# A trunk of two layers on one core: raw weights, the place of a mean and the staging of the output in the last projection

## The chip, the core and the metric

The kernel runs on one core of a Trainium2 chip. The metric is the device time of one execution in microseconds (us). It is given as the median of three runs, beside the span of one profiled execution, which is the time from its first instruction to its last.

## What is computed

The reference is a trunk of two residual layers over 512 tokens with 16 meta tokens in front, D = 2048, all in float32. Layer 0 holds a convolution module beside sparse attention, layer 1 a gated linear recurrence with 16 heads. The change lies in the end of layer 1 and in the last norm. Cut to that:

```python
o = hgrn2_chunkwise(q, log_f, k, v)                 # 16 heads of 128
o = o * rsqrt(mean(o*o, -1) + 1e-6) * norm_g        # per head
o = o.reshape(b, t, 2048) * silu(g)                 # g = hn @ w_in's last quarter
h = h + o @ w_out                                   # the output projection
return rms_norm(h, final_norm_gain)[:, 16:]         # over D, meta tokens dropped
```

## The kernel before

Everything is kept transposed, with 128 channels on the partitions and tokens along the free dimension. A product in float32 accuracy is made from three matmuls: weights and activations are each split into a high part (rounded, made by ScalarE with an activation) and a low part (the rest, made by VectorE with a subtraction), and high x high, low x high and high x low go into the same PSUM tile. `products` (L170) issues these for eight contraction steps of 128: L174, L175 and L176.

**Weights.** `load_half` (L140) brings 128 x 1024 raw weights (512 KB) into a tile `w32` from the queue of SP, splits it into `wh` (L146, ScalarE) and `wl` (L147, VectorE) and returns both. There are two buffers of `w32` and three each of `wh` and `wl`. In the trace `w32` is named `w`.

**Layer 1's gate.** The loop at L968 makes 16 stripes of the gate (`stripe(S_G + h)`), and multiplies each head's result `ON[h]` by it (`gate_on`, L937). A head's tile holds 512 tokens, seen as two halves of 256 (HS).

**The output projection by Strassen's scheme.** The 2048 x 2048 projection is done for pairs `pr` of output tiles n0 = 2 pr and n1 = 2 pr + 1, over two halves of the contraction (heads 0 to 7 and 8 to 15) and two halves of the tokens, c = 0 and 1. The scheme (Winograd's variant) takes seven products instead of eight: m = 1 to 7. Each product has its own weights (a slice of w, or a sum of slices, `wsum`, that was made in DRAM earlier) and its own form of the activations, named in FORM (L911): B11, B21 and N1 are split early, as the gate proceeds (`early_form`, L919, tiles `eh` and `el`, 28 buffers each); N2 for heads 4 to 7, T3, B22 and T4 are split late (`late_form`, L924) into the tiles `xh` and `xl` that held layer 1's input, and N2 for heads 0 to 3 early. A head's `ON` tile is read by the late forms last.

**The turns.** The list `turns` (L1039) has 56 entries (pr, m). A turn is one product: 24 matmuls of 256 columns into one PSUM tile (`mps` or `s1`, which the trace calls `s`), whose weights come from `weights` (L979). The first ten turns are (0, 1), (0, 5), (0, 2), (0, 6), (1, 1), (1, 5), (0, 7), (0, 3), (0, 4), (1, 2); pairs 6 and 7 alternate at the end with m = 1, 6, 7, 2, 4, 5, 3, so the last six turns are (6, 4), (7, 4), (6, 5), (7, 5), (6, 3), (7, 3). With m = 1 the two residual tiles `H2[n0]` and `H2[n1]` (256 KB each) are loaded from DRAM (L1050) into the ring `on` of 16 buffers that held ON. After each product VectorE adds it to H2 (`add`, L989; m = 6 and 7 go through a sum U).

**Norm and output.** When a tile's half is complete, `finish` (L993) squares it on ScalarE (L1003), adds the square to `acc2` (named `rstd` in the trace, L1005), and scales the tile by the gain (L1006). When the 16th tile of a token half is done, `final` (L1010) is called at once: a matmul with a matrix of 1/D over `acc2` and one over the last square (L1016, L1017, in plain float32) give the mean in every partition; ScalarE makes Ln and Exp (L1019, L1021) after a table load (L1014); VectorE multiplies the 16 tiles (L1033) into staging tiles, and SP sends these out (L1034). The first half (c = 0) stages in pieces of two tiles through `gt2` (two buffers, named `gt`); the second in pieces of 4, 4, 4, 2, 2 in buffers of `w32`, `wh` and `wl`.

**What sets the order.** Each engine and each DMA queue takes its instructions in the order of the program. This order is made when the kernel is built, by a planner with a timeline of its own: among what it holds to be ready it takes the highest level first (`band`: weights 5, evacuation 4, side work 3, products 0). `tc.issue_after(i)` keeps instructions of the engine of `i` behind `i`. A tile's buffer is taken again when all its readers are done.

Of the kernel before, what the change touches and what calls it, by code (L numbers as in the profile page):

```python
# [10 lines left out]
F32 = mybir.dt.float32  # L11
F32R = mybir.dt.float32r
# [6 lines left out]
SEQ = 512  # L19
NM = 16  # L20
T = SEQ + NM
HT = T // 2
D = 2048
KT = D // 128
# [48 lines left out]
def trunk_kernel(ctx: ExitStack, tc: tile.TileContext, x: bass.AP, w: bass.AP, wukv: bass.AP,  # L73
# [3 lines left out]
    V, S, G, P, Q = nc.vector, nc.scalar, nc.gpsimd, nc.tensor, nc.sync  # L77

    def band(level):
        return tc.high_priority(level * 1000000)  # L80

    WGT, EVAC, SIDE, CONV = 5, 4, 3, 2

    consts = ctx.enter_context(tc.tile_pool(name="consts", bufs=1, side="left"))
    wpool = ctx.enter_context(tc.tile_pool(name="wpool", bufs=3, side="left"))
# [7 lines left out]
    def ps1():  # L93
        return side_ps.tile([128, 512], F32, name="s1", bufs=4)
# [15 lines left out]
    def ones_of(val, name):  # L110
        t = cst([128, 128], F32, name)
        V.memset(t, val)
        return t

    ones_d = ones_of(1.0 / D, "ones_d")
# [21 lines left out]
        V.tensor_scalar(vec[:, V_RG:V_RG + 16], vec[:, V_RG:V_RG + 16], 0.5, None, op0=OP.mult)  # L137


    def load_half(src, pool=wpool, names=("wh", "wl"), bufs=3, m=128):  # L140
        w32 = wpool.tile([128, 1024], F32, name="w32", bufs=2)
        Q.dma_start(w32, src)
        hi = pool.tile([128, 1024], F32R, name=names[0], bufs=bufs)
        lo = pool.tile([128, 1024], F32R, name=names[1], bufs=bufs)
        used, uh, ul = [t.rearrange("p (k m) -> p k m", m=128)[:, :, :m] for t in (w32, hi, lo)]
        S.activation(uh, used, AF.Copy)  # L146
        V.tensor_tensor(ul, used, uh.bitcast(F32), op=OP.subtract)  # L147
        return hi, lo
# [20 lines left out]

    def products(o, hi, lo, X, start, stop, m=128):  # L170

        for k, (xh, xl) in enumerate(X):
            ws = slice(k * 128, k * 128 + m)
            P.matmul(o, hi[:, ws], xh, start=start and k == 0, stop=False)  # L174
            P.matmul(o, hi[:, ws], xl, start=False, stop=False)  # L175
            P.matmul(o, lo[:, ws], xh, start=False, stop=stop and k == 7)  # L176

    def evac(dst, parts, rstd):
        o = T - dst.shape[-1]
# [58 lines left out]
    last = {}  # L238
# [64 lines left out]
    for k in range(KT):  # L303
        xh, xl = X0[k]
        st, sp = k == 0, k == KT - 1
        for parts, s, m in ((kwp, S_KW, KWM), (c0p, S_C, 128)):
            hi, lo = first[s, k // 8]
            ws = slice(k % 8 * m, k % 8 * m + m)
# [5 lines left out]
    with band(EVAC):  # L314
        for k in range(KT):
# [5 lines left out]
            else:  # L321
                sq = et([128, T], F32, "sq", 3)
# [13 lines left out]
    for j in range(2):  # L336
        ps = c0p if j == 0 else stripe(S_C + 1, X0, got=first, ring=(ps1, ps1))
        c = et([128, T], F32, "gb", 2)
        with band(EVAC):
            evac(c, ps, rstd0)  # L340
        with band(SIDE):
            sq = et([128, T], F32, "sq", 3)
# [4 lines left out]
    with band(SIDE):  # L347
        p = ps1()
# [16 lines left out]
    with band(SIDE):  # L365
# [7 lines left out]
        for o in range(0, BL, 352):  # L373
# [3 lines left out]
            p = ps1()  # L377
# [48 lines left out]
    for t in range(NB):  # L426
        m = et([128, wk(t)], F32, f"mask{t}", 1)
# [170 lines left out]
    for step in EVEN:  # L598
        what, i = step[0], int(step[1:])
# [34 lines left out]
    r2p = r2.__enter__()  # L634
# [5 lines left out]
    for n in range(KT):  # L640
# [4 lines left out]
        with band(EVAC):  # L645
# [6 lines left out]
            else:  # L652
                sq = U.tile([128, T], F32, name="sq1", bufs=2)
                last = S.activation(sq, hin, AF.Square)
# [16 lines left out]
    def ht(shape, dt, name, bufs=1):  # L671
        return (hp if name == "on" else hrp).tile(shape, dt, name=name, bufs=bufs)
# [225 lines left out]
    fp = ctx.enter_context(tc.tile_pool(name="fp", bufs=2, side="left", reuse_waits="tile"))  # L898
    HS = SEQ // 2
# [11 lines left out]
    FORM = {1: "B11", 2: "B21", 3: "B22", 4: "T4", 5: "N1", 6: "N2", 7: "T3"}  # L911
    forms = {f: [None] * 8 for f in FORM.values()}
# [4 lines left out]
        V.tensor_tensor(lo, src, hi.bitcast(F32), op=OP.subtract)  # L917

    def early_form(name, i, src):  # L919
        hi, lo = [fp.tile([128, HS], F32R, name=n, bufs=28) for n in ("eh", "el")]  # L920
        split2(hi, lo, src)
        forms[name][i] = hi, lo

# [10 lines left out]
    def gt2():  # L934
        return fp.tile([128, 2 * SEQ], F32, name="gt2", bufs=2)
# [22 lines left out]
    def forms_of_both(i):  # L958

        a, b, aj, bj = quarters(i)  # L960
        early_form("B21", i, aj)
        V.tensor_tensor(b, bj, b, op=OP.subtract)
        V.scalar_tensor_tensor(a, b, -1.0, a, op0=OP.mult, op1=OP.subtract)
        if i < 4:
            early_form("N2", i, a)
        V.scalar_tensor_tensor(aj, a, -1.0, aj, op0=OP.mult, op1=OP.subtract)

    for i in range(8):  # L968
# [3 lines left out]
                forms_of(i)  # L972
    with band(SIDE):
        for name in ("N2", "T3", "B22", "T4"):
            for i in range(4 if name == "N2" else 0, 8):
                late_form(name, i)


    def weights(pr, m):  # L979

        n = S_OO + 2 * pr
        src = {1: w[n, 0], 2: w[n, 1], 4: w[n + 1, 1]}[m] if m in (1, 2, 4) else wsum[pr, m]
        return load_half(src)

    H2 = [None] * KT
    acc2 = r2p.tile([128, T], F32, name="rstd1", bufs=1)[:, :SEQ]
    done = [0, 0]

    def add(n, c, ps, op=OP.add):  # L989
        h2 = H2[n][:, c * HS:(c + 1) * HS]  # L990
        V.tensor_tensor(h2, h2, ps, op=op)

    def finish(n, c):  # L993

        cs = slice(c * HS, (c + 1) * HS)
        h2, a2 = H2[n][:, cs], acc2[:, cs]
        done[c] += 1
        sq = last = None
        if done[c] == 1:
            S.activation(a2, h2, AF.Square)  # L1000
        else:
            sq = tmp()
            last = S.activation(sq, h2, AF.Square)  # L1003
            if done[c] < KT:
                V.tensor_tensor(a2, a2, sq, op=OP.add)  # L1005
        S.activation(h2, h2, AF.Identity, scale=col(V_GF + n))  # L1006
        if done[c] == KT:
            final(c, sq, last)

    def final(c, sq, last):  # L1010
        tk = slice(c * HS, (c + 1) * HS)
        if c == 0:
            with tc.issue_after(last.ins):
                S.preload_act_table_set("natural_log_exp_and_others")  # L1014
        p = ps1()[:, :HS]
        P.matmul(p, ones_d, acc2[:, tk], start=True, stop=False)  # L1016
        P.matmul(p, ones_d, sq, start=False, stop=True)  # L1017
        rs = tmp()
        S.activation(rs, p, AF.Ln, bias=eps_r)  # L1019
        rsp = ps1()[:, :HS]  # L1020
        S.activation(rsp, rs, AF.Exp, scale=-0.5)  # L1021
        with band(0 if c else SIDE - EVAC):
            at = 0
            for g, size in enumerate((4, 4, 4, 2, 2) if c else (2,) * 8):
                if c == 0:
                    o = gt2()
                elif g < 2:
                    o = wpool.tile([128, 1024], F32, name="w32", bufs=2)
                else:
                    o = wpool.tile([128, 1024], F32R, name=("wh", "wl", "wh")[g - 2], bufs=3).bitcast(F32)  # L1030
                o = o[:, :size * HS].rearrange("p (n t) -> p n t", n=size)
                for i in range(size):
                    V.tensor_tensor(o[:, i, :], H2[at + i][:, tk], rsp, op=OP.mult)  # L1033
                Q.dma_start(out[at:at + size, :, tk].rearrange("n p t -> p n t"), o)  # L1034
                at += size


    TWO = 6
    turns = [(pr, m) for pr in range(TWO) for m in (1, 5, 2, 6, 7, 3, 4)]  # L1039
    turns[4:9] = [(1, 1), (1, 5), (0, 7), (0, 3), (0, 4)]  # L1040
    turns += [(pr, m) for m in (1, 6, 7, 2, 4, 5, 3) for pr in (6, 7)]

    U = {}
    for at, (pr, m) in enumerate(turns):
        n0, n1 = 2 * pr, 2 * pr + 1
        if m == 1:
            with band(EVAC):
                for n in (n0, n1):
                    H2[n] = ht([128, SEQ], F32, "on", 16)
                    Q.dma_start(H2[n], h1d[n, :, NM:])  # L1050
        o = (mps if at % 7 < 3 else ps1)()[:, :HS]
        with band(WGT):
            hi, lo = weights(pr, m)
        products(o, hi, lo, forms[FORM[m]], True, True)
        with band(EVAC):
            if m == 1:
                u = U[pr] = fp.tile([128, HS], F32, name="u", bufs=2)
                S.activation(u, o, AF.Copy)
                add(n0, 0, o)
            elif m == 5:  # L1060
                add(n0, 1, o)
                add(n1, 1, o, OP.subtract)
                if pr >= TWO:
                    finish(n1, 1)
            elif m == 2:
                add(n0, 0, o)
                finish(n0, 0)
            elif m == 6:
                V.tensor_tensor(U[pr], U[pr], o, op=OP.add)
                add(n0, 1, U[pr])  # L1070
            elif m == 7:
                V.tensor_tensor(U[pr], U[pr], o, op=OP.add)
                h2 = H2[n1].rearrange("p (c t) -> p c t", c=2)
                V.tensor_tensor(h2, h2, U[pr][:, None, :].to_broadcast([128, 2, HS]), op=OP.subtract)
                if pr < TWO:
                    finish(n1, 1)
            elif m == 3:
                add(n0, 1, o)
                finish(n0, 1)
            else:  # L1080
                add(n1, 0, o, OP.subtract)
                finish(n1, 0)
    r2.__exit__(None, None, None)


# [88 lines left out]
```

## Time and profile before

| | us |
|---|---|
| median of three runs (lowest to highest) | 1967.5 (1965.49 to 1968.01) |
| the profiled execution, its own time | 1964.9 |
| its span | 1962.4 |
| TensorE busy | 1931.9 |
| VectorE busy | 1355.2 |
| ScalarE busy | 846.4 |

How to read it: the span is 2.5 us shorter than the execution's own time, which includes what lies around the first and the last instruction. Busy is the time in which an engine runs at least one instruction; matmuls overlap, so two of them can start 0.12 us apart and each last 0.28 us. Times in the rows below are counted from the span's start. The projection's turns begin at 1766.9 us.

### The profile page before, as it was taken

How to read it: one execution, taken by the hardware profiler on the slowest of the kernel's cores; microseconds unless marked ns; L12 is line 12 of the kernel's file. 1: busy time of each engine (PE TensorE's matmuls, PEld its weight loads, DVE VectorE, ACT ScalarE, POOL GpSimd, SP SyncE). 2: the span in 40 equal slices, each digit the busy share in tenths (PEclk: the TensorE clock that was granted, in tenths of full speed). 3: DMA queues.
4: the chain of work that ended last, by engine and by line, in shares of the span. 5: the costliest groups of instructions: out<-in, count | busy, mean ns of one | idle time of the engine just before them, and what ended most of it. 6: DMA issues, size and time to landing. Idle time of an engine off the chain costs nothing.

```text
span 1962.4 us, 36435 instructions
## 1 busy us (share of the span) xinstructions
PE 1931.9 (98%) x14998; PEld 1818.5 (93%) x14998; DVE 1355.2 (69%) x2581; ACT 846.4 (43%) x1475; POOL 119.4 (6%) x202
## 2 busy tenths in 40 slices
PE   9999999999999999999999999999999999999996
PEld 8999899999999999999999999999999988889995
DVE  6699989987376454344777777777777756557665
ACT  6332442234435433233455545454545443345443
POOL 1000000111120100001001000010000000000000
PEclk9999999999999999999999999999999999999998
DMA  6322323334342443434445444344444422235554
GB/s 210 108 83 95 102 88 105 104 99 131 101 115 87 115 137 132 141 135 152 136 130 140 125 123 119 119 140 128 131 119 119 119 76 97 97 118 205 173 172 161
DMA packets 77270, 244.59 MB, mean 125 GB/s; under 512 B 9712, under 2 KB 17432, under 8 KB 76592
## 3 DMA queue, kind: packets, MB, share of 16 engines
q1 hardware_dynamic: 62624, 194.21, 29.4%
q0 software_dynamic: 14192, 47.86, 10.9%
q8 instruction: 118, 1.93, 0.4%
q14 instruction: 48, 0.39, 0.1%
q10 hardware_dynamic: 288, 0.19, 0.0%
HBM read 223.12 MB, written 44.78 MB: 137 GB/s over the span
## 4 chain that ended last, share of the span: by engine, by line
PE 73%; DMA 5%; DVE 3%; ACT 2%; issue 1%; ACTq 0%; DVEq 0%
PE mps L176 21%; PE mps L174 21%; PE mps L175 21%; DMA w<-ws 3%; DMA w<-in_w_dram 2%; ACT wh L146 1%; DVE wl L147 1%; PE po L547 1%; PE s L522 1%; PE s L716 1%; PE s L715 1%; PE s L717 1%; PE po L838 1%; PE po L837 1%; PE s L834 1%
## 5 line engine op out<-in xcount | busy, mean ns | idle before, releaser
L174 PE MATMUL mps<-xh,wh 128*128 128x264 f32 (+2 forms) x3492 | 1070.6, 307 | 3.9 <-DVE gt L181 2.2
L176 PE MATMUL mps<-xh,wl 128*128 128x264 f32 (+2 forms) x3492 | 1072.2, 307 | 0.1
L175 PE MATMUL mps<-xl,wh 128*128 128x264 f32 (+2 forms) x3492 | 1070.3, 307 | 0.1
L174 PEld LDWEIGHTS mps<-xh,wh 128*128 128x128 f32 x3492 | 658.4, 189 | 33.5 <-DVE gt L181 2.2
L175 PEld LDWEIGHTS mps<-xl,wh 128*128 128x128 f32 x3492 | 657.3, 188 | 30.5 <-issue 0.6
L176 PEld LDWEIGHTS mps<-xh,wl 128*128 128x128 f32 x3492 | 657.4, 188 | 28.0 <-DVE wl L147 0.5
L146 ACT ACTIVATE wh<-w 128x1024 fp32r<-128x1024 f32 x313 | 331.5, 1059 | 608.6 <-PE mps L175 452.8
L147 DVE TENSOR_TENSOR wl<-w,wh 128x1024 fp32r<-128x1024 f32 x313 | 382.8, 1223 | 229.7 <-ACT wh L146 224.7
L492 DVE SCALAR_TENSOR_TENSOR z<-u,vec,z 128x528 f32<-128x528 f32 x240 | 180.5, 762 | 2.6
L181 DVE TENSOR_TENSOR gt<-mps,rstd 128x264 f32<-128x264 f32 (+1 forms) x80 | 38.5, 482 | 74.1 <-PE mps L176 73.1
L711 ACT ACTIVATE qhm<-q 128x256 f16<-128x256 f32 x128 | 51.8, 417 | 56.4 <-DVE q L813 44.2
L798 DVE COPY_PREDICATED A<-msk,s 128x256 f32<-128x256 uint8 x96 | 46.5, 484 | 28.3 <-PE s L717 27.8
L176 PE MATMUL s<-xh,wl 128*128 128x256 f32 (+1 forms) x220 | 63.0, 286 | 1.2 <-DVE wl L147 1.1
L712 DVE SCALAR_TENSOR_TENSOR qlm<-q,qhm 128x256 f16<-128x256 f32 x128 | 52.9, 424 | 15.8 <-ACT qhm L711 15.7
L174 PE MATMUL s<-xh,wh 128*128 128x256 f32 (+1 forms) x220 | 62.2, 283 | 0.3 <-ACT wh L146 0.3
L175 PE MATMUL s<-xl,wh 128*128 128x256 f32 (+1 forms) x220 | 62.0, 282 | 0.0
L176 PE MATMUL mps<-eh,wl 128*128 128x256 f32 x156 | 45.2, 290 | 1.8 <-DVE wl L147 1.6
L457 ACT ACTIVATE sq<-s 128x264 f32<-128x264 f32 (+3 forms) x80 | 29.2, 393 | 38.9 <-PE s L455 32.3
L647 DVE TENSOR_TENSOR hin<-mps,hin 128x264 f32<-128x264 f32 x32 | 13.8, 433 | 46.4 <-PE mps L176 46.4
L711 ACT ACTIVATE kt1h<-k 128x256 f16<-128x256 f32 x64 | 26.5, 414 | 44.4 <-DVE k L804 44.4
L174 PE MATMUL mps<-eh,wh 128*128 128x256 f32 x156 | 44.2, 283 | 0.4 <-ACT wh L146 0.4
L823 ACT ACTIVATE kk<-s 128x512 f32<-128x512 f32 x16 | 9.6, 600 | 81.1 <-PE s L821 81.1
(356 smaller groups left out, 2600.8 us busy)
## 6 DMA issues: line engine op xcount, KB each, us to landing
w<-in_w_dram SPq DMA_DIRECT2D x283, 512.0 KB, 3.7
ws<-in_w_dram POOLq DMA_DIRECT2D x48, 512.0 KB, 5.6
w<-ws SPq DMA_DIRECT2D x32, 512.0 KB, 3.6
ws<-ws POOLq DMA_DIRECT2D x16, 512.0 KB, 5.1
hin<-in_x_dram SPq DMA_DIRECT2D x16, 264.0 KB, 3.7
h1d<-hin SPq DMA_DIRECT2D x16, 264.0 KB, 2.1
on<-h1d SPq DMA_DIRECT2D x16, 256.0 KB, 4.7
z<-in_x_dram SPq DMA_DIRECT2D x8, 264.0 KB, 4.6
```

The costliest lines, as they stand in the source:

```text
L146: S.activation(uh, used, AF.Copy)
L147: V.tensor_tensor(ul, used, uh.bitcast(F32), op=OP.subtract)
L174: P.matmul(o, hi[:, ws], xh, start=start and k == 0, stop=False)
L175: P.matmul(o, hi[:, ws], xl, start=False, stop=False)
L176: P.matmul(o, lo[:, ws], xh, start=False, stop=stop and k == 7)
L181: V.tensor_tensor(dst[:, sl.start - o:sl.stop - o], p[:dst.shape[0]], rstd[:dst.shape[0], sl], op=OP.mult)
L457: S.activation(r[:, :s1 - s0], p[:, :s1 - s0], AF.Relu)
L492: eng.scalar_tensor_tensor(z, u[:, j:j + T], col(V_CW + i * CW + j), z, op0=OP.mult, op1=OP.add)
L522: P.matmul(p[:nq, :s1 - s0], qh[:, q0:q0 + nq], Kh[:, s0:s1], start=True, stop=True)
L711: S.activation(hi, src, AF.Copy, scale=scale)
L712: V.scalar_tensor_tensor(lo, src, scale, hi, op0=OP.mult, op1=OP.subtract)
L798: V.copy_predicated(A.rearrange("p b (n a m) -> p b n a m", a=2, m=mm)[:, :, :, 1, :], msk[:, li - 1 + i:li + i, :].rearrange("p b (n m) - ...
```

## The change

- `load_half` can be given a raw tile. In the projection every third load (`loads[0] % 3 == 0`) takes a tile `w33` from the pool `fp` instead of a buffer of `w32`.
- `early_form` has 24 buffers instead of 28, and the form N2 is split late for all eight heads.
- The residual tiles of pair 0 go to two buffers of their own (`h2`) instead of the ring `on`.
- The first 14 turns are (0, 1), (0, 5), (0, 2), (1, 1), (1, 5), (1, 2), (0, 6), (1, 6), (0, 7), (1, 7), (0, 3), (1, 3), (0, 4), (1, 4); the others stay.
- `final` is no longer called by `finish`. For the first half it is called in turn (7, 5), and its first matmul is kept behind `issued[3]`, the last matmul of that turn's fourth contraction step; for the second half it is called after the loop.
- The first half stages through eight tiles `xh` and `xl` of the forms' pool; the second half in pieces of 1, 1, 2, 4, 4, 2, 2 in `gt2`, `gt2`, `wh`, `w32`, `w32`, `wl`, `wh`.

```diff
-    def load_half(src, pool=wpool, names=("wh", "wl"), bufs=3, m=128):
-        w32 = wpool.tile([128, 1024], F32, name="w32", bufs=2)
+    def load_half(src, pool=wpool, names=("wh", "wl"), bufs=3, m=128, w32=None):
+        w32 = w32 or wpool.tile([128, 1024], F32, name="w32", bufs=2)
...
+        issued = []
         for k, (xh, xl) in enumerate(X):
...
-            P.matmul(o, lo[:, ws], xh, start=False, stop=stop and k == 7)
+            issued.append(P.matmul(o, lo[:, ws], xh, start=False, stop=stop and k == 7))
+        return issued
...
-        hi, lo = [fp.tile([128, HS], F32R, name=n, bufs=28) for n in ("eh", "el")]
+        hi, lo = [fp.tile([128, HS], F32R, name=n, bufs=24) for n in ("eh", "el")]
...
-        if i < 4:
-            early_form("N2", i, a)
...
-            for i in range(4 if name == "N2" else 0, 8):
+            for i in range(8):
                 late_form(name, i)
...
-        return load_half(src)
+        loads[0] += 1
+        return load_half(src, w32=fp.tile([128, 1024], F32, name="w33", bufs=1) if loads[0] % 3 == 0 else None)
...
         if done[c] == KT:
-            final(c, sq, last)
+            pending.append((sq, last))
 
-    def final(c, sq, last):
+    def final(c, behind=None):
+        sq, last = pending.pop()
...
-        P.matmul(p, ones_d, acc2[:, tk], start=True, stop=False)
+        with tc.issue_after(behind.ins) if behind else ExitStack():
+            P.matmul(p, ones_d, acc2[:, tk], start=True, stop=False)
...
-            for g, size in enumerate((4, 4, 4, 2, 2) if c else (2,) * 8):
+            for g, size in enumerate((1, 1, 2, 4, 4, 2, 2) if c else (2,) * 8):
                 if c == 0:
+                    o = r2p.tile([128, T], F32R, name=("xh", "xl")[g % 2], bufs=KT).bitcast(F32)
+                elif g < 2:
                     o = gt2()
-                elif g < 2:
+                elif size == 4:
                     o = wpool.tile([128, 1024], F32, name="w32", bufs=2)
                 else:
-                    o = wpool.tile([128, 1024], F32R, name=("wh", "wl", "wh")[g - 2], bufs=3).bitcast(F32)
+                    o = wpool.tile([128, 1024], F32R, name="wl" if g == 5 else "wh", bufs=3).bitcast(F32)
...
-    TWO = 6
-    turns = [(pr, m) for pr in range(TWO) for m in (1, 5, 2, 6, 7, 3, 4)]
-    turns[4:9] = [(1, 1), (1, 5), (0, 7), (0, 3), (0, 4)]
+    turns = [(pr, m) for ms in ((1, 5, 2), (6,), (7,), (3,), (4,)) for pr in (0, 1) for m in ms]
+    turns += [(pr, m) for pr in range(2, 6) for m in (1, 5, 2, 6, 7, 3, 4)]
     turns += [(pr, m) for m in (1, 6, 7, 2, 4, 5, 3) for pr in (6, 7)]
...
-                    H2[n] = ht([128, SEQ], F32, "on", 16)
+                    H2[n] = fp.tile([128, SEQ], F32, name="h2", bufs=2) if pr == 0 else ht([128, SEQ], F32, "on", 16)
...
-        products(o, hi, lo, forms[FORM[m]], True, True)
+        issued = products(o, hi, lo, forms[FORM[m]], True, True)
         with band(EVAC):
+            if (pr, m) == (7, 5):
+                final(0, issued[3])
...
+    with band(EVAC):
+        final(1)
```

## Rows read from the trace of the kernel before

**Rows 1.** The page, part 1: busy time, share of the span, instructions.

```profile
PE 1931.9 (98%) x14998; PEld 1818.5 (93%) x14998; DVE 1355.2 (69%) x2581; ACT 846.4 (43%) x1475; POOL 119.4 (6%) x202
```

**Rows 2.** Busy time by stretch: stretch, length, each engine's, granted clock, DMA share, GB/s.

```profile
core 0: us, PE busy (x) PEld busy (x) DVE busy (x) ACT busy (x) POOL busy (x), PEclk, DMA share, GB/s
1766.90:1780.00 13.10, 12.08 (x98) 11.68 (x97) 11.39 (x24) 6.59 (x12) 0.00 (x0) 1.00 0.74 263
1780.00:1928.20 148.20, 143.68 (x1152) 138.77 (x1152) 92.86 (x142) 71.90 (x106) 0.00 (x0) 1.00 0.53 174
1934.90:1939.00 4.10, 4.10 (x21) 4.01 (x20) 1.64 (x5) 1.83 (x4) 0.00 (x0) 0.54 0.12 40
```

**Rows 3.** Timeline of TensorE's matmuls, first and 46th of a run (start, duration).

```profile
1814.80 0.28 PE L174 MATMUL mps<-eh,wh 128*128 128x256 f32 x1
...
1820.18 0.28 PE L174 MATMUL s<-eh,wh 128*128 128x256 f32 x1
```

**Rows 4.** Waits (total, times, longest): ScalarE, VectorE from 1780; ScalarE 1640 to 1750.

```profile
ACT wh L146 <- DMA w<-ws: 41.4, 24, 3.1
ACT wh L146 <- DMA w<-in_w_dram: 28.5, 18, 3.3
...
DVE u L1069 <- PE s L176: 1.5, 2, 1.3
...
ACT wh L146 <- PE mps L175: 48.3, 18, 4.5
```

**Rows 5.** The chain that ended last, in order of time: start, duration, what.

```profile
1820.50 3.45 DMA w<-ws
1824.04 1.07 ACT wh L146
1825.13 1.22 DVE wl L147
1826.38 3.47 DMA w<-in_w_dram
```

**Rows 6.** Timeline of TensorE around the two means; idle time before, its releaser.

```profile
1928.09 0.27 PE L176 MATMUL mps<-xh,wl 128*128 128x256 f32 x1
1931.73 1.16 PE L1016 MATMUL s<-rstd,ones_d 128*128 128x256 f32 x2 [3.38 <-DVE rstd L1005]
1934.23 1.22 PE L1017 MATMUL s<-t,ones_d 128*128 128x256 f32 x2 [1.33 <-ACT t L1003]
1934.89 0.78 PE L174 MATMUL s<-eh,wh 128*128 128x256 f32 x1
...
1948.15 0.59 PE L1016 MATMUL s<-rstd,ones_d 128*128 128x256 f32 x2
```

**Rows 7.** Timelines around the opening (ScalarE, SP, TensorE), and the weight loads' landing times.

```profile
1757.87 2.69 ACT L916 ACTIVATE xh<-on 128x256 fp32r<-128x256 f32 x8
...
1767.23 3.53 SPq L1050 DMA_DIRECT2D on<-h1d  x7
...
1779.83 0.39 PE L174 MATMUL s<-eh,wh 128*128 128x256 f32 x1 [1.02 <-ACT wh L146]
...
DMA to landing us min/median/max: 3.3/3.6/6.2
```

**Rows 8.** Timelines of SP, ScalarE and VectorE towards the end.

```profile
1922.07 9.62 SPq L142 DMA_DIRECT2D w<-ws  x4
...
1932.81 1.06 ACT L146 ACTIVATE wh<-w 128x1024 fp32r<-128x1024 f32 x1 [1.88 <-DMA w<-ws]
...
1949.29 0.42 DVE L1033 TENSOR_TENSOR gt<-on,s 128x256 f32<-128x256 f32 x1 [1.28 <-DMA out_dram<-gt]
1949.62 0.41 DVE L991 TENSOR_TENSOR on<-on,s 128x256 f32<-128x256 f32 x1
```

**Rows 9.** The second half's output: timelines of VectorE and SP, busy time of one microsecond.

```profile
1952.20 2.74 DVE L1033 TENSOR_TENSOR w<-on,s 128x256 f32<-128x256 f32 x8 [1.83 <-ACT s L1021]
...
1953.64 1.70 SPq L1034 DMA_DIRECT2D out_dram<-w  x2
...
1955.00:1956.00 1.00, 0.00 (x0) 0.00 (x0) 1.00 (x4) 0.00 (x0) 0.00 (x0) 0.50 1.02 333
```

## What the change does to the time, predicted

> **What bounds the kernel now.** The page comes first: TensorE is busy for 98% of the span [rows 1], so only time in which it idles or crawls can be won. The change touches the last 195 us alone, so next I cut these into stretches: the opening and the long stretch of the projection, 52 turns up to 1928.2 us, and what follows its stop [rows 2]. One turn is 24 matmuls of 256 columns. Where nothing waits, 45 of them go by between 1814.80 and 1820.18 us, 0.1196 us each [rows 3]; I use 0.119, so a turn is 2.86 us. The long stretch holds 1152 matmuls, 137.1 us at that pace, and took 148.2: 11.1 us are lost. The opening holds 98, 11.7 us, and took 13.1: 1.4 us lost.
>
> Who waits there? Not TensorE in large pieces: ScalarE's split of the raw weights waits for a load 42 times, 69.9 us together [rows 4], while in the stage before, whose turns are longer, the same instruction waits for TensorE. The chain of waits shows the loop [rows 5]: load 3.45 us, ScalarE's high part 1.07, VectorE's low part 1.22, and only then is the raw buffer free for its next load: 5.88 us around. With two buffers that is 2.94 us a turn, just over TensorE's 2.86; with the longer landings the stretch averages 148.2 / 48 = 3.09.
>
> The end is a second, separate loss. After the last product of turn (7, 4) TensorE meets the mean of the first token half (L1016, L1017): it waits 3.38 us for the sum of squares and 1.33 for the last square, and its next product starts at 1934.89, 6.8 us after the one before [rows 6]. Behind the stop the granted clock is 0.54 for 4 us, its lower level for most of it [rows 2].
>
> **Part 1: the third raw buffer (w33).** The loop of 5.88 us now serves three turns, 1.96 a turn. Even with a landing of 6.2 us, the longest of this part [rows 7], it is 8.5 / 3 = 2.8, still under 2.86. So TensorE becomes the bound, with ScalarE's split waiting for it as in the stage before. The split weights keep three buffers: the split for turn j+3 waits for the end of turn j, then needs 1.07 + 1.22 us plus at most a few adds of 0.4, and is due 5.7 us after that end: about 2.5 us of cover. VectorE (92.9 us busy of 148.2) and ScalarE (71.9) would be at 68% and 52% of 137 us, and DMA at 0.53 of its time would go to 0.57 [rows 2]. The saving lies between 0 (the loads can't come faster) and 12.5 (both losses gone). I take 11.1, the whole loss of the long stretch, and leave the opening's 1.4 in place, since the rows nearest to the new loop are the stage before, where no such wait reaches TensorE.
>
> A word on the size. Over the long stretch matmuls are busy 143.68 us of 148.20, weight loads 138.77 [rows 2]. The Trainium skill (Perfetto Trace Analysis, Identifying the Most-Contended Engine) says that matmul busy time misjudges the headroom since matmuls overlap, and that the busy share of weight loads is the better measure. By matmul busy time this part would be worth 4.5 us, by weight loads 9.4; my count of starts gives 11.1, so here the trace sides with the rule.
>
> **Part 2: opening order and forms.** The first two pairs now run 1, 5, 2 each before 6, 7, 3, 4 alternately. The same 56 products run; the N2 form is due at turn 6 instead of 3, T3 at 8 instead of 6, B22 at 10 instead of 7. Four N2 forms move from the gate stage to the late queue (ScalarE's high part takes 2.69 us for eight, 0.34 each [rows 7]; with VectorE's low part, taken to be as long, four are 2.7 us); three more turns (8.6 us) hide them, and without that cover they cost at most 1.4 us on VectorE, which is busy 11.39 of 13.1 us here [rows 2]. H2 of pair 0 gets its own buffers: two loads of 256 KB leave the queue behind the ON tiles on SP. What could be late next is DMA: today seven H2 loads go out at 1767.23, a weight load takes up to 6.2 us to land against a median of 3.6, and TensorE waits 1.02 us for a split [rows 7]. The third buffer sends each weight load one turn earlier. Bounds: gain 1.4, loss 5.5 (below); I take 0.
>
> **Part 3: the mean of the first half later.** Four fp32 matmuls, the table load, Ln, Exp, sixteen products on VectorE and eight output DMAs move behind the fourth contraction step of turn (7, 5), that is behind 36 products, 36 x 0.119 = 4.3 us after the end of (7, 4). On SP no weight load is passed: the last four went out by 1931.7 [rows 8], in step with the turns, and the third buffer sends them earlier still. The sum was ready 3.6 us after that end and the last square 6.1 us after it [rows 6]; the square came late because ScalarE stood 1.88 us before a split whose load had not landed [rows 8]. With loads on time I expect the square 1.2 to 2.5 us after the end, so there is no stop and no lower clock. From 1928.09 to the mean of the second half at 1948.15 took 20.06 us [rows 6]; 96 products and two more pairs of fp32 pieces at 0.59 would take 11.4 + 1.2 = 12.6. Saving 7.4; if the old lags stay, a stop of 1.8 us remains, saving 5.6.
>
> **Part 4: staging.** For the first half eight tiles of the finished forms replace two buffers. Today VectorE stands in order behind an output DMA (1.28 us) and only then does the last add of (7, 3), at 1949.62 [rows 8], though its product ended about 1948.4: 1.2 us of the final chain, gone unless the add lands behind a product of the first half (0.34 us each). For the second half the products start 2.6 us after the last add [rows 8, 9]. Taking 2.2 us from the start of the first half's mean to its products (an estimate: the 2.6 less the add), VectorE has from 4.3 + 2.2 = 6.5 us after (7, 4) to 12.6 + 0.3 + 2.6 = 15.5 for sixteen products (2.74 for eight [rows 9], 5.5) and eight adds and sums (at 0.34, 2.7): 8.2 of 9.0 us, so it fits. For the second half pieces of 1, 1, 2 precede the fours: the first output issue came at 1953.64, four products after their start; now it comes after one, 1.0 us earlier [rows 9]. DMA runs at its full share and 333 GB/s from 1955 on [rows 9], so its end moves with its start: 0.9 us (bounds 0 and 1.0).
>
> **Sum.** 11.1 + 0 + 7.4 + 1.2 + 0.9 = 20.6 us. On the profiled execution of 1964.9 us (span 1962.4 and 2.5 around it) that gives 1944.3; that execution is 2.6 under the median of the runs, 1967.5, and against the median it gives **1947** us.
>
> **Rivals.**
> 1. *The loads stay the bound.* If what limits them is not the buffer but DMA or SP's order, Part 1 is nil and the end's 9.5 remain: 1958. Against: a load every 2.86 us is 183 GB/s, and the same engines move 333 at full share [rows 9]. For: landings stretch when loads overlap. Chance 0.09.
> 2. *The end keeps part of its stop.* The order on each in-order engine is planned ahead; if the square stays behind a split (1.8 us), and the sixteen products, now squeezed, run into the second half's chain (1 to 3 us), 4 us are given back: 1951. Chance 0.17.
> 3. *The opening burst.* H2 loads become free in two bunches and go out on the queue of the weights. Seven of 256 KB are 1.84 MB, 5.5 us at 333 GB/s, and a weight load issued behind them lands that much later; today the opening lost 1.4 us in all. If a bunch falls before the loads of turns 3 to 5 the whole of it shows: 1952. Chance 0.08. The Trainium skill (DMA: Bandwidth & Descriptors, Queues, rings and completion order) says that each DMA engine takes the descriptors of a ring in ring order; by that rule a third load on the same ring passes nothing, and the longest landing here, 6.2 us, agrees.
> 4. *Slower.* VectorE is in order. If the plan puts the low part for the next turn behind an add that waits for the running turn's last matmul, TensorE stops for add 0.41 + low part 1.22 less its first two matmuls 0.24, some 1.4 us with the handoffs. It decides against the change from 15 of the 56 turns on (20.6 / 1.4); at 24 turns (three in seven) it is 34 us: 1981. Before, VectorE's largest entry of this kind is 2 waits, 1.5 us, in 148 us [rows 4], which speaks against it. Chance 0.05.
> 5. *The change does not do what it says*: w33 or the new order buys nothing and the end's stop is only moved, within 4 us of before. Chance 0.03.
>
> **How the numbers follow.** The forecast has 0.58. Its own range: everything won (22.1) from the lowest run, 1965.5, is 1943.4; with the opening's loss tripled (2.8 more) and the end's lags kept (1.8) it is 1951.6. For 8 in 10 the range reaches up to rival 1: 1943 to 1958. A measurement of this kernel tells 0.2%, 3.9 us, from no change, so faster means under 1963.6: forecast, rivals 1 to 3, 0.92, less 0.02 for several of them at once: 0.90. Same: rival 5 and that 0.02, 0.05. Slower: rival 4, 0.05.
>
> **What would show it.** Part 1 right: in the long stretch ScalarE's split waits for TensorE, not for a load, and 1152 matmuls take 137 to 139 us. Wrong: the waits for loads stay near 70 us. Part 2: no wait of 1 us or more in TensorE's first 14 turns. Part 3: no gap over 0.5 us around L1016, and a granted clock of 1.00 through the last four turns. Part 4: the last add within 0.5 us of the last product, and some 13 us instead of 14.2 from the second half's mean to the end. The forecast is wrong if VectorE's low parts stand behind adds that wait for TensorE, or if SP holds weight loads behind H2 loads.

## The result and the profile after

The changed kernel takes 1945.3 us (median of four runs, 1944.4 to 1945.4) beside 1966.6 for the kernel before (four runs now, three of them those given above, 1965.5 to 1968.0): a ratio of 0.989, 95% interval 0.9873 to 0.9908, 21.3 us less. The forecast was 1947. The profiled execution took 1945.34 us, its span 1943.1.

Busy time by stretch, cut at the same products as [rows 2]; then the four turns after the long stretch, and the rest:

```profile
core 0: us, PE busy (x) PEld busy (x) DVE busy (x) ACT busy (x) POOL busy (x), PEclk, DMA share, GB/s
1768.36:1780.05 11.69, 11.69 (x99) 11.69 (x98) 11.09 (x23) 4.89 (x9) 0.00 (x0) 1.00 1.02 357
1780.05:1917.40 137.35, 136.91 (x1153) 136.71 (x1153) 99.67 (x150) 77.58 (x115) 0.00 (x0) 1.00 0.61 188
1917.40:1929.80 12.40, 12.40 (x102) 12.11 (x100) 10.07 (x25) 6.71 (x11) 0.00 (x0) 1.00 0.33 109
1929.80:1943.10 13.30, 1.16 (x5) 0.68 (x4) 6.66 (x20) 2.60 (x6) 0.00 (x0) 0.62 0.64 216
```

The long stretch has gone from 148.2 to 137.35 us for the same products, the opening from 13.10 to 11.69, and the granted clock (the share of TensorE's full 2.4 GHz that it was given; its lower level, 1.2 GHz, is 0.50) stays at 1.00 to the last turn. ScalarE's waits from 1780 to 1915 (total, times, longest) have changed their releaser, which is what ended them, as against [rows 4]: no wait for a load is left.

```profile
ACT wh L146 <- PE s L176: 31.8, 25, 4.5
ACT wh L146 <- PE mps L176: 27.0, 20, 1.8
```

The timeline of TensorE around the two means (L1021 and L1022 here), as [rows 6]:

```profile
1917.27 0.28 PE L177 MATMUL mps<-xh,wl 128*128 128x256 f32 x1
...
1921.70 0.59 PE L1021 MATMUL s<-rstd,ones_d 128*128 128x256 f32 x2
1922.13 0.59 PE L1022 MATMUL s<-t,ones_d 128*128 128x256 f32 x2
1922.37 0.47 PE L175 MATMUL s<-eh,wh 128*128 128x256 f32 x1
...
1929.54 0.28 PE L177 MATMUL s<-xh,wl 128*128 128x256 f32 x1
1931.12 0.70 PE L1021 MATMUL s<-rstd,ones_d 128*128 128x256 f32 x2 [1.30 <-DVE rstd L1008]
```

The stop of 6.8 us behind turn (7, 4) is gone: the first mean stands among the products of turn (7, 5) without a wait. But the second half's mean, which waited for nothing at its sum before, now waits 1.30 us for it. VectorE's timeline says why (L994 is an add, L1008 adds a square to the sum):

```profile
1925.35 0.74 DVE L994 TENSOR_TENSOR on<-on,s 128x256 f32<-128x256 f32 x2
1926.02 0.41 DVE L1041 TENSOR_TENSOR xh<-on,s 128x256 f32<-128x256 f32 x1
...
1929.00 0.74 DVE L1041 TENSOR_TENSOR xl<-on,s 128x256 f32<-128x256 f32 x2
1929.66 0.41 DVE L994 TENSOR_TENSOR on<-on,s 128x256 f32<-128x256 f32 x1
...
1930.33 0.41 DVE L994 TENSOR_TENSOR on<-on,s 128x256 f32<-128x256 f32 x1
1930.66 0.41 DVE L1008 TENSOR_TENSOR rstd<-rstd,t 128x256 f32<-128x256 f32 x1
```

Between 1926.02 and 1929.66 stand eleven products of the first half (L1041), and the adds of turns (6, 3) and (7, 3) come behind them.

For the whole projection a table from TensorE's and VectorE's timelines, each number the distance between two starts (the last column runs to the end of the span): the first 14 turns; turns 15 to 52; from the last product of turn 52 to that of turn 56; from there to the second half's first output product; from there to the end. It has all kernels of the study but the two with a slowed load. It counts from the projection's first product, because that one starts at 1766.6 to 1769.7 us in these profiles, in the two above 1.5 us apart: 0.8 of it is there by 720 us and 0.7 comes at about 734 us, in layer 0. Each row is one execution. Turns 15 to 52 agree within 0.04 us in all nine kernels with the third buffer, but spread over 1.7 us in the three without it, so in those a difference of that size in the table may be chance.

| kernel | 14 turns | 38 turns | last 4 | to output | to end | sum |
|---|---|---|---|---|---|---|
| before | 42.94 | 118.25 | 19.95 | 4.16 | 10.17 | 195.5 |
| changed | 40.66 | 108.25 | 12.27 | 3.68 | 9.85 | 174.7 |
| only_w33 | 41.53 | 108.28 | 13.45 | 5.36 | 10.16 | 178.8 |
| no_w33 | 45.06 | 119.96 | 13.29 | 7.35 | 9.85 | 195.5 |
| only_mean | 42.71 | 119.05 | 13.68 | 7.62 | 10.36 | 193.4 |
| mean_at_once | 40.66 | 108.25 | 14.02 | 2.90 | 9.84 | 175.7 |
| mean_65 | 40.66 | 108.25 | 12.25 | 3.58 | 9.88 | 174.6 |
| stage_gt2 | 41.20 | 108.25 | 12.27 | 7.76 | 10.13 | 179.6 |
| old_opening | 41.83 | 108.25 | 12.27 | 3.91 | 9.85 | 176.1 |
| w33_staging | 41.53 | 108.28 | 14.05 | 2.90 | 10.20 | 177.0 |
| pieces_44422 | 40.66 | 108.25 | 12.27 | 3.68 | 10.17 | 175.0 |
| pieces_2 | 40.64 | 108.25 | 12.27 | 3.68 | 9.57 | 174.4 |

### The profile page after: what moved, and what is told of

Read it like the earlier page. It is cut to its first block, busy times and chain, and to the rows that moved or that the text cites. A ratio compares the mean times of both kernels' runs of the same rounds, so it can differ in the third digit from the quotient of the medians.

```text
span 1943.1 us, 36429 instructions
## 1 busy us (share of the span) xinstructions
PE 1922.4 (99%) x14998; PEld 1813.8 (93%) x14998; DVE 1357.0 (70%) x2581; ACT 846.7 (44%) x1475; POOL 119.4 (6%) x202
## 4 chain that ended last, share of the span: by engine, by line
PE 80%; DVE 1%; DMA 0%; ACT 0%; issue 0%; DVEq 0%
PE mps L177 22%; PE mps L175 22%; PE mps L176 22%; PE s L176 1%; PE s L177 1%; PE s L175 1%; PE po L549 1%; PE s L524 1%; PE s L718 1%; PE s L717 1%; PE s L719 1%; PE po L840 1%; PE po L839 1%; PE s L836 1%; PE s L420 1%; PE s L407 0%
## 5 line engine op out<-in xcount | busy, mean ns | idle before, releaser
L176 PE MATMUL s<-xl,wh 128*128 128x256 f32 (+1 forms) x240 | 67.7, 282 | 0.0
L175 PE MATMUL s<-xh,wh 128*128 128x256 f32 (+1 forms) x240 | 67.5, 281 | 0.0
L177 PE MATMUL s<-xh,wl 128*128 128x256 f32 (+1 forms) x240 | 67.4, 281 | 0.0
L176 PEld LDWEIGHTS s<-xl,wh 128*128 128x128 f32 x240 | 45.1, 188 | 0.6 <-issue 0.6
L175 PEld LDWEIGHTS s<-xh,wh 128*128 128x128 f32 x240 | 45.2, 188 | 0.0
L177 PEld LDWEIGHTS s<-xh,wl 128*128 128x128 f32 x240 | 45.2, 188 | 0.0
```

The lines of the kernel that those rows point to most:

```text
L177: issued.append(P.matmul(o, lo[:, ws], xh, start=False, stop=stop and k == 7))
```

## The experiments

**The third buffer alone** (only_w33):

```diff
+        loads[0] += 1
+        return load_half(src, w32=fp.tile([128, 1024], F32, name="w33", bufs=1) if loads[0] % 3 == 0 else None)
-        hi, lo = [fp.tile([128, HS], F32R, name=n, bufs=28) for n in ("eh", "el")]
+        hi, lo = [fp.tile([128, HS], F32R, name=n, bufs=26) for n in ("eh", "el")]
-        if i < 4:
+        if i < 2:
```

> The kernel before with the third raw buffer alone (two of the four early N2 forms are split late to make room); nothing else of the change. Theory (the raw buffers' loop bounds the long stretch, and the late loads also made the last square late): the long stretch falls from 148.2 us to 137 to 139, ScalarE's split waits for TensorE there, and the stop at the first half's mean shrinks from 6.8 us to 2.5 to 3.5, though the mean has not moved: 1966.6 - 11 - 3.5 to 5 = 1951 to 1953. Rival (loads bound by DMA or by SP's order): the long stretch stays over 145 us and the time within 3 us of before. Rival (the opening's order was needed): the opening still loses 1 us or more.

Measured: 1949.3 us, ratio 0.9904 (0.9887 to 0.9921), 18.8 us less than before. ScalarE's waits, 1785 to 1915, and the first mean (L1019, L1020):

```profile
ACT wh L146 <- PE s L175: 28.1, 24, 1.8
ACT wh L146 <- PE mps L175: 24.4, 19, 1.8
...
1919.64 0.67 PE L1019 MATMUL s<-rstd,ones_d 128*128 128x256 f32 x2
1921.14 0.70 PE L1020 MATMUL s<-t,ones_d 128*128 128x256 f32 x2 [0.83 <-ACT t L1006]
1921.49 0.47 PE L174 MATMUL s<-eh,wh 128*128 128x256 f32 x1
```

The loop's bound is lifted, 10.0 us in turns 15 to 52. And the mean, which stands where it stood before, no longer stops TensorE for 6.8 us: its wait is 0.83, and the last four turns take 6.5 us less. The next product starts at 1921.49, so the stop is 2.0 us (2.5 to 3.5 expected), and the time is 1.7 us below the expected range. So one cause, the late loads, made both losses. The opening still loses: 41.53 against 40.66, as the second rival had it, though by 0.9 us only.

**All but the third buffer** (no_w33):

```diff
-        return load_half(src, w32=fp.tile([128, 1024], F32, name="w33", bufs=1) if loads[0] % 3 == 0 else None)
+        return load_half(src)
```

> The changed kernel with every load in the two buffers of w32; all else as changed. Theory: the long stretch is back at about 148 us and the square's lag with it, so 11 to 13 us are lost: 1956 to 1959. Rival (the order of the opening and the residual's own buffers carried the gain): within 3 us of the changed kernel, 1945 to 1948.

Measured: 1964.8 us, ratio to before 0.9983 (0.9974 to 0.9993); the table's sum is that of the kernel before, but the profile is the longest of its ten runs (1966.7). A miss of 6 us: the loss against the changed kernel is not 11 to 13 but 19.5 (18.3 by the two ratios, as the runs were made at different times). The long turns are slow again as expected, and a new wait stands at the second mean:

```profile
1951.45 1.22 PE L1021 MATMUL s<-rstd,ones_d 128*128 128x256 f32 x2 [4.03 <-DVE rstd L1008]
```

The loads come late, with them the last splits on VectorE, with them the first half's sixteen products, and the second half's adds behind these. What the later mean saves in the last four turns (6.7 us) is given back in this profile, but only half of it there: 3.2 us on the way to the output, 2.1 in the first 14 turns and 1.7 in the long ones. In the opening TensorE waits 2.3 us for a split, and its clock is at its lower level for 3.4 us from 1783.8.

**The mean's place alone** (only_mean):

```diff
         if done[c] == KT:
-            final(c, sq, last)
+            pending.append((sq, last))
+            if (pr, m) == (7, 5):
+                final(0, issued[3])
+    with band(EVAC):
+        final(1)
```

> The kernel before with the first half's mean behind the fourth contraction step of turn (7, 5), nothing else. Theory (the lags of late loads stay): the sum is there, the last square comes about 6.1 us after (7, 4), so a stop of about 1.8 us is left of 4.7 us of waits, the clock stays up, and 5 to 6 us are saved: 1961. Rival (the place alone is enough): no stop, 7.4 us saved: 1959. Rival (the stop only moves): 1965 to 1967.

Measured: 1964.5 us, ratio 0.998 (0.9971 to 0.9989): 3.6 us, between the theory and the third rival. The timeline of TensorE:

```profile
1936.39 0.59 PE L1022 MATMUL s<-rstd,ones_d 128*128 128x256 f32 x2
1937.24 0.70 PE L1023 MATMUL s<-t,ones_d 128*128 128x256 f32 x2 [0.26 <-ACT t L1005]
...
1948.00 1.22 PE L1022 MATMUL s<-rstd,ones_d 128*128 128x256 f32 x2 [2.98 <-DVE rstd L1007]
```

The stop at the first mean is down to 0.26 us, less than the 1.8 expected, so the place does what it should; but a wait of 2.98 us comes up at the second mean, and the way to the output grows by 3.5. Part of this is the old staging: VectorE stands 1.25 us for an output landing before the second half's last adds.

**The mean at its old place in the changed kernel** (mean_at_once):

```diff
             pending.append((sq, last))
+            if c == 0:
+                final(0)
-            if (pr, m) == (7, 5):
-                final(0, issued[3])
```

> The changed kernel with the first half's mean called again as soon as its 16th tile is squared, so that it stands right behind turn (7, 4). Theory (loads on time): the square is there 1.6 us after (7, 4), so TensorE stops for 1.5 to 2 us, without a lower clock; the sixteen products then start some 2.5 us earlier and the second half's mean no longer waits 1.3 us for its sum: 1944.5 to 1947, no difference that can be told. Rival (the place was worth its 6 us by itself): a stop of 5 us or more and a lower clock behind it: 1950 to 1953.

Measured: 1946.3 us, ratio to before 0.9891 (0.9876 to 0.9906), beside 0.989 for the change: no difference that can be told. The wait for the last square at the first mean, and at the second:

```profile
1917.58 0.70 PE L1024 MATMUL s<-t,ones_d 128*128 128x256 f32 x2 [0.84 <-ACT t L1006]
...
1931.23 0.70 PE L1024 MATMUL s<-t,ones_d 128*128 128x256 f32 x2 [0.53 <-ACT t L1006]
```

The last square lands 1.6 us after the last product of (7, 4), as expected; the table shows 1.75 us more in the last four turns and 0.78 less behind them. With loads on time, the mean's place is worth 1 us in the profiles, which the times can't tell.

**A longer loop** (slow_before, slow_after), in the projection alone:

```diff
         Q.dma_start(w32, src)
+        if again:
+            G.dma_start(w32[:, :256], src[:, :256])
```

> The kernel before, where each raw weight tile of the projection gets a second, small load (256 of its 1024 columns, 128 KB, over GpSimd's queue) behind the first: the loop of a raw buffer grows by one more landing, 2 to 3 us, while the bytes grow by a quarter. Theory (loop over number of buffers): 7.9 to 8.9 us over two buffers are 3.95 to 4.45 us a turn instead of 3.1, over 56 turns 45 to 75 us more: 2010 to 2040. Rival (bytes or a queue bind, not the buffer): 640 KB a turn at 333 GB/s are 2.0 us, nothing more: 1967 to 1975.

> The changed kernel with the same second small load. Theory (loop over number of buffers): 7.9 to 8.9 us over three buffers are 2.6 to 3.0 us a turn against TensorE's 2.86, so almost all is hidden: 1945 to 1955. Rival (the second load costs by its bytes or its queue): the same increase as the kernel before shows with it, 45 us or more.

Measured: 2050.7 us (ratio 1.0425, 1.0404 to 1.0446) and 1987.4 (1.0103, 1.0083 to 1.0123): 83 us more on two buffers, 42 on three. Both are above what was expected, the second by 32 us: the third buffer halves the loss and does not hide it. Busy time in the long stretch, two buffers, then three, and loads of 1790 to 1930 with their median time to landing, from issue to all data there, in us (SP's are the first loads, GpSimd's the second ones):

```profile
1790.00:1930.00 140.00, 107.80 (x708) 101.90 (x707) 59.09 (x88) 45.48 (x66) 15.61 (x29) 0.86 0.45 139
...
w<-ws SPq DMA_DIRECT2D x16, 512.0 KB, 3.5
w<-in_w_dram SPq DMA_DIRECT2D x13, 512.0 KB, 4.1
w<-ws POOLq DMA_DIRECT2D x17, 128.0 KB, 2.5
```

```profile
1790.00:1900.00 110.00, 98.72 (x761) 95.42 (x760) 61.37 (x94) 48.48 (x72) 16.63 (x31) 0.96 0.59 190
...
w<-ws SPq DMA_DIRECT2D x23, 512.0 KB, 4.5
w<-in_w_dram SPq DMA_DIRECT2D x18, 512.0 KB, 4.5
w<-ws POOLq DMA_DIRECT2D x23, 128.0 KB, 2.9
```

A turn of 24 takes 140 / 708 x 24 = 4.75 us on two buffers, 110 / 761 x 24 = 3.47 on three. The chain that ended last on two buffers shows the loop:

```profile
1836.36 3.73 DMA w<-in_w_dram
1840.16 0.50 issue
1840.66 2.83 DMA w<-in_w_dram
1843.52 1.07 ACT wh L148
1844.61 1.24 DVE wl L149
```

From 1836.36 to the end at 1845.85 it is 9.5 us: 9.5 / 2 = 4.75. With three, 4.5 + 0.5 + 2.9 and the same splits (2.3) and handoffs (0.1) are 10.3: 3.4.

On two buffers that is one round of the loop. Over all loads of the two stretches, from one issue into a buffer to the next, the trace gives a mean of 9.66 us on two buffers and 10.60 on three, 4.83 and 3.53 a turn, and almost nothing in it stands idle: the split begins 0.10 and 0.17 us after the second landing. So the form holds, loop over number of buffers. In the same way the kernel before gives 6.24 us with 0.10 idle, 3.12 a turn, and the changed kernel 8.40 us, of which the split waits 2.2 for TensorE.

The rival is out in both its halves: 139 GB/s is less than the kernel before moved [rows 2], and GpSimd's load goes out 0.6 us after the first has landed in both kernels. TensorE's clock is lower here (0.86 and 0.96), and on two buffers the chain runs over TensorE's products for about a fifth of 1790 to 1900; but since the loop has hardly any idle time, the clock does not set the turn. What was mis-sized is the loop: the second load adds 3.3 us, not 2 to 3, and with the second loads on three buffers each load takes longer, which is the piece of rival 1 that is true. In the changed kernel itself it is not: the median landing is 3.6 us, as before.

**The first half staged in two buffers** (stage_gt2):

```diff
-                    o = r2p.tile([128, T], F32R, name=("xh", "xl")[g % 2], bufs=KT).bitcast(F32)
+                    o = gt2()
```

> The changed kernel with the first half's output staged through the two buffers of gt2 again. Theory: VectorE stands behind output DMAs with the second half's last adds behind it; with the products 6 us later than before, that hits the chain in full: 2 to 4 us slower, 1947.5 to 1949.5. Rival (the sixteen products fit between the landings): within 1 us of the changed kernel.

Measured: 1949.3 us, ratio 0.991 (0.9894 to 0.9927), 4.0 us over the change's median. The timeline of VectorE:

```profile
1933.31 1.57 DVE L1041 TENSOR_TENSOR gt<-on,s 128x256 f32<-128x256 f32 x4 [1.63 <-DMA out_dram<-gt]
1937.09 0.42 DVE L1041 TENSOR_TENSOR gt<-h,s 128x256 f32<-128x256 f32 x1 [2.21 <-DMA out_dram<-gt]
```

The waits for landings sit in front of the second half's output, and the way to it is 7.76 us instead of 3.68. The place is not quite the one expected: the last add is on time here, it is the products behind it that wait.

**The mean earlier still** (mean_65):

```diff
-            if (pr, m) == (7, 5):
-                final(0, issued[3])
+            if (pr, m) == (6, 5):
+                final(0, issued[5])
```

> The changed kernel with the first half's mean behind the sixth contraction step of turn (6, 5), 18 products behind (7, 4) instead of 36. Theory (what is left at the end is VectorE's line of sixteen products, ahead of the second half's last adds): the square is there after 1.6 us and the mean at 2.1 us, so no stop there; the products start 2.1 us earlier and the 1.3 us wait of the second half's mean goes: 0.5 to 1.5 us faster than the changed kernel, 1944 to 1945. Rival (the place in TensorE's order matters only by the stop): the same time within 0.3 us.

Measured: 1945.2 us, ratio 0.9888 (0.9873 to 0.9903). The rival: nothing changes. The products begin at 1923.33 instead of 1923.69, since VectorE has the last split of the weights to do first, and the adds of turns (7, 5), (6, 3) and (7, 3) then stand behind all sixteen.

**The opening and the pieces.** First the old turns and residual buffers in the changed kernel (old_opening):

```diff
+    turns = [(pr, m) for pr in range(6) for m in (1, 5, 2, 6, 7, 3, 4)]
+    turns[4:9] = [(1, 1), (1, 5), (0, 7), (0, 3), (0, 4)]
...
-                    H2[n] = fp.tile([128, SEQ], F32, name="h2", bufs=2) if pr == 0 else ht([128, SEQ], F32, "on", 16)
+                    H2[n] = ht([128, SEQ], F32, "on", 16)
```

> The changed kernel with the old order of the first two pairs and all residual tiles in the ring on again (all N2 forms stay late). Theory: the kernel before with the third buffer alone still lost some 3 us in its first 14 turns, waiting for forms and for a load behind residual loads; that comes back here: 1947 to 1949. Rival (the third buffer alone covers the opening): within 1 us of the changed kernel.

The kernel of only_w33 with the eight staging tiles (w33_staging):

```diff
-                    o = gt2()
+                    o = r2p.tile([128, T], F32R, name=("xh", "xl")[g % 2], bufs=KT).bitcast(F32)
```

> The kernel before with the third raw buffer (two of the four early N2 forms late) and the eight staging tiles for the first half, nothing else: the mean at once, the old opening, the old pieces of the second half. Theory (the buffer and the staging are the change, the mean's place is not): 1.5 to 3 us under the third buffer alone, 1946.5 to 1948, and within 3 us of the whole change. Rival (the staging only counts where the mean stands late): no better than the third buffer alone, 1949 to 1950.

The changed kernel with the second half's old pieces (pieces_44422), and with small ones throughout (pieces_2):

```diff
-            for g, size in enumerate((1, 1, 2, 4, 4, 2, 2) if c else (2,) * 8):
+            for g, size in enumerate((4, 4, 4, 2, 2) if c else (2,) * 8):
```

```diff
-            for g, size in enumerate((1, 1, 2, 4, 4, 2, 2) if c else (2,) * 8):
+            for g, size in enumerate((1, 1, 2, 2, 2, 2, 2, 2, 1, 1) if c else (2,) * 8):
```

> The changed kernel with the second half sent out in pieces of 4, 4, 4, 2, 2 again. Theory (the first output goes out 1 us earlier, but DMA then runs dry before the first piece of 4): 0.2 to 0.5 us slower in the span behind the second half's Exp, no difference in the time. Rival (DMA's end moves with its start): 0.9 us slower.

> The changed kernel with the second half sent out in pieces of 1, 1, six of 2, 1, 1, in ten buffers. Theory: DMA no longer runs dry at 1936 and the last piece is 128 KB, so the last landing comes 0.5 to 1.0 us earlier: 1944.3 to 1944.9. Rival (the issues of more pieces hold it up): no gain.

Measured, in this order: 1947.5 (0.9892, 0.9876 to 0.9909), 1946.8 (0.9894, 0.9879 to 0.9909), 1945.6 (0.9885, 0.987 to 0.99) and 1944.5 (0.988, 0.9866 to 0.9895). No interval tells any of the four from the change; the profiles do. The opening is worth 1.2 us in its 14 turns, less than expected (its 3 us seem to be counted from 1766.9, but in the profile of only_w33 the projection starts at 1769.7): TensorE's weight loads wait there 1.8 us for a split, 0.6 with the new order. The buffer and the staging alone come within 2.3 us of the change in the table's sum and are 1.8 under the buffer alone, as the theory had it. Pieces of 4, 4, 4, 2, 2 cost 0.3 us, as expected; pieces of 1 and 2 throughout win 0.3, less than the 0.5 to 1.0 expected; the changed kernel's DMA runs dry once before its first piece of four, in the fourth of these microseconds:

```profile
1933.00:1934.00 1.00, 0.00 (x0) 0.00 (x0) 0.78 (x3) 0.19 (x1) 0.00 (x0) 0.50 0.02 8
1934.00:1935.00 1.00, 0.00 (x0) 0.00 (x0) 1.00 (x4) 0.00 (x0) 0.00 (x0) 0.50 0.40 132
1935.00:1936.00 1.00, 0.00 (x0) 0.00 (x0) 1.00 (x4) 0.00 (x0) 0.00 (x0) 0.50 0.80 269
1936.00:1937.00 1.00, 0.00 (x0) 0.00 (x0) 1.00 (x4) 0.00 (x0) 0.00 (x0) 0.50 0.42 148
1937.00:1938.00 1.00, 0.00 (x0) 0.00 (x0) 1.00 (x4) 0.00 (x0) 0.00 (x0) 0.50 1.03 345
```

## Why the prediction was right, and where it was not

The time is right and so is the sum from the projection's start: 20.6 forecast, 195.5 - 174.7 = 20.8 in the profiles (the spans differ by 19.3, because of the later start). That the sum is so close is in part luck: Part 2 won 1.4 us that were not forecast, and Part 3 missed 1.2. And the parts are not what each edit won: the third buffer alone won 195.5 - 178.8 = 16.7 us, where Part 1 had 11.1.

- *Part 1, right.* 11.1 forecast for the long stretch, 148.2 - 137.35 = 10.85 measured; the idle time of matmuls (4.5) would have missed it by more than half. That of weight loads (9.4) comes nearer. The releaser changed as said. Rival 1 falls with only_w33. The Trainium skill (Perfetto Trace Analysis, Identifying the Most-Contended Engine) ranks the busy share of weight loads above matmul busy time; the trace agrees, 9.4 being nearer to 10.85 than 4.5.
- *Part 2, sized wrong.* 0 forecast, 1.4 measured, the upper bound: with the third buffer alone the first 14 turns still take 0.9 us longer than in the changed kernel, and the new order wins that. No burst (rival 3) came: the largest wait of TensorE in its first 14 turns is 0.44 us.
- *Part 3, right in place and wrong in its cause and size.* From the last product of (7, 4) to the second mean it took 13.85 us instead of 20.06, 6.2 won of 7.4. The failed step is the bookkeeping: the text itself said that the late square came from late loads, and yet put the whole stop to the mean's new place. only_w33 removes the stop without moving the mean, and mean_at_once loses 1 us by moving it back. The stop came from the late loads, which Part 1 ends. Part 1 and Part 3 each remove it alone, 6.5 and 6.3 us of the last four turns (of the 6.3, 3.5 are lost again on the way to the output); together they win 7.7, not their sum.
- *The 1.2 us that Part 3 misses* are the new wait of 1.30 us at the second mean, rival 2's second half. The step that failed is the capacity sum of Part 4: VectorE's work does fit in the 9 us, but it is in order, and the second half's adds wait behind eleven products. "8.2 of 9.0 us, so it fits" looked at the amount and not at the order, and its window was too long: the adds are due at the second half's mean, 12.6 us after (7, 4), not at 15.5, and from 6.5 to 12.6 there are 6.1 us for 8.2 us of work in order. Without the third buffer the wait at this place is 2.98 us (only_mean, with the old staging) and 4.03 us (no_w33).
- *Part 4, right in sum, 2.1 forecast, 2.3 measured from the second mean to the end (14.21 us before, 11.94 after; the sign, some 13 us, counted only the 1.2 of the last add).* Its first half is confirmed at a higher price: with the mean late, two buffers cost 4.0 us, though it is the first half's products and not the last add that wait. Its second half was too large: 0.9 forecast, 0.3 measured, because DMA's start moved but it then ran dry. The last add starts 0.8 us after the last product does, not within 0.5.
- *Rival 4* did not come: VectorE's waits for a product are short ones (0.7 us at most), and TensorE's matmuls wait once before the end of (7, 4), for 0.44 us.

What stays open: why the projection starts up to 3 us apart in these profiles; no run was made for it. The traces show one piece: in five of the twelve (only_w33, no_w33, only_mean, mean_65, old_opening) the granted clock is at its lower level for 3.4 us at about 736 us, and 1.2 to 1.5 us are lost there against the kernel before. Why it falls in these and not in the others is not shown.

## What to carry to other kernels

A ring of buffers is read as its loop over its number: add the landing and every step up to the buffer's release, divide by the buffers, and compare with the consumer's turn. When the quotient is near the turn, the consumer's losses look small and scattered (0.2 to 1 us here), and the larger stop somewhere behind them may be the same lag coming due; book a stop under its cause, not under the edit that happens to move past it. And when work is moved later on an in-order engine, look not only whether it fits but what is then queued behind it.

## What the runs showed of the hardware that was not expected

Loads landed later where more of them overlap: with three raw buffers and the second loads (slow_after) the 512 KB loads take 4.5 us (median) against 3.5 to 4.1 with two (slow_before), at a DMA share of only 0.59. Three buffers alone do not do it: in the changed kernel a buffer is loading for 3.8 of 8.4 us (7.4 of 10.6 in slow_after), and the median stays at 3.6. And TensorE's granted clock, which changed between its two levels, averaged 0.86 over a stretch of slow_before in which the engine was busy 107.80 of 140 us, with stops of 3 us at most; in the kernel before, busy 143.68 of 148.20 us, it stayed at 1.00 [rows 2].
